# One 512-column projection per token tile in the attention heads of a hybrid encoder, in place of two of 256

## The chip, the cores and the metric

The kernel runs on one core of one Trainium2 chip. The metric is device time in microseconds (us) of one execution of the whole program; the median of several runs is compared.

## The reference

The reference is an encoder trunk of two layers on 1024 tokens of width 1024, in float32. Each layer normalises its input, projects it to 8192 columns at once, and runs three groups of heads on parts of them: four mLSTM heads, six HGRN2 heads and four differential-attention heads. Each group's output is multiplied by a SiLU gate of its own, and an output projection adds to the residual stream. The change touches the projection of the attention heads only:

```python
h = rms_norm(x, norm_g[l])
proj = jnp.einsum("bsd,de->bse", h, w_in[l])
(xm, om, zm, hq, hff, hfb, hi, hz, aq, ak, av, az) = jnp.split(proj, split_pts, axis=-1)
...
ao = differential_attention(aq..., ak..., av..., lam, positions)
ao = head_rms_norm(ao, a_norm_g[l], A_HEADS) * (1.0 - lam_init)
y_a = ao * jax.nn.silu(az)
```

An attention head takes 128 columns each of aq (two query sets of 64), ak (two key sets of 64), av (values) and az (gate). Queries and keys get a rotary embedding on 16 of their 64 dimensions. The head's weights are softmax(Q1 K1) - lam softmax(Q2 K2), and they multiply V.

## The kernel before, in words

**Precision by three products.** Float32 products are formed from a rounded part and a remainder in the type fp32r. The normalised input h lies transposed in SBUF as `hh` (high) and `hl` (low), each in two halves of 512 tokens. A weight block is fetched by `load_w` in pieces of 128x512 (DMA on SP's queue into a raw buffer, three of them), copied to `whi` by ScalarE (L136) and subtracted to `wlo` by GpSimd (L137). The pool `wp` has two slots of 2048 columns each for `whi` and `wlo`; a slot is given out again when everything that reads it is done. A block of up to 256 columns fills one slot with all eight k (k counts the 128-row pieces of the 1024 input channels). A wider block is split: k 0 to 3 in one slot, k 4 to 7 in the next.

**Token projection.** `proj_token` (L308) gives one token tile (128 tokens) of a block: 24 matmuls, 8 k times hh*whi, hh*wlo, hl*whi, the token tile as loaded weights and the block's columns as moving data. They add up in one of two PSUM banks (tag `pj`), and `evac` empties the bank.

**Attention.** After the other groups' heads, head 0's projection runs by itself. Then for each head the loop over eight query tiles `qt` computes scores S (L997, L998), the row maxima (L1000), exponentials (L1004), the combination of the two softmaxes (L1013), eight transposes (L1018), the product with V (L1025), and the gated output into the head's gate buffer (L1028). The projection of the next head is a Python generator, `a_proj`, and `next(nxt, None)` at the end of each query step takes one piece of it. Before the change it has eight pieces of two tiles each: aqk tiles 0, 1; aqk 2, 3; avz 0, 1; avz 2, 3; and the same for the second half of the tokens. With the second aqk piece of a half comes `qk_half`: rotary embedding on VectorE (L931 to L937), 16 transposes (L942), and copies to the query and key tiles `qks` (L944 to L948), from a buffer `qk` of which there is one.

**Buffers.** Values `v` (traced as av) and gates `gt` (traced as ag) have two buffers each, so head h+2 takes head h's. Head h's gate buffer is in use until `o_post`, traced in the second query step of the head after it, has normalised (L913) and transposed it (L918, L919).

**Order.** The tile framework decides, when the kernel is built, in which order each engine executes its instructions: by program order among those that its own timeline has ready. It also places the waits for slots. On the chip each engine then follows its list.

**After attention.** The output projection (L1064, traced as op) loads `w_out` through the same pool `wp`, and its y tiles through the same raw buffers. Its first three groups of channels need no attention output, and their matmuls fill in beside the softmax of head 3.

Of the kernel before, what the change touches and what calls it, by code (L numbers as in the profile page):

```python
# [13 lines left out]
AF = mybir.ActivationFunctionType  # L14
ALU = mybir.AluOpType
AX = mybir.AxisListType

P = 128
# [22 lines left out]
def _cols(start, n):  # L41
    return list(range(start, start + n))


def w_blocks():
    blocks = {}
    order = []

    def add(name, cols):
        blocks[name] = cols  # L50
        order.append(name)

    for i in range(3):
        add(("xm", i), _cols(XM + i * 256, 256))
    for j in range(6):
        add(("zm", j), _cols(ZM + j * P, P))
    for p in range(2):
        add(("om", p), _cols(OM + p * 384, 384))
    for h in range(HH):
        add(("hqf", h), _cols(HQ + h * P, P) + _cols(HFF + h * P, P))  # L60
        add(("hfb", h), _cols(HFB + h * P, P))
        add(("hiz", h), _cols(HI + h * P, P) + _cols(HZ + h * P, P))
    for h in range(AH):
        add(("aqk", h), _cols(AQ + h * P, P) + _cols(AK + h * P, P))
        add(("avz", h), _cols(AV + h * P, P) + _cols(AZ + h * P, P))
    return blocks, order


# [22 lines left out]
def trunk(ctx, tc, x_in, positions, w_in, w_out, pvec, rvec, out, dbg=None):  # L91
    nc = tc.nc
# [47 lines left out]
    def load_win(l, name):  # L140
        n = len(W_BLOCKS[name])
        o = W_OFF[name] * 8
        ks_per = 8 if n <= 256 else 4
        parts = []
        for k0 in range(0, 8, ks_per):
            hi, lo = load_w(w_in[l, :, o + k0 * n:o + (k0 + ks_per) * n], ks_per * n)
            for k in range(ks_per):
                parts.append((hi[:, k * n:(k + 1) * n], lo[:, k * n:(k + 1) * n]))
        return parts
# [197 lines left out]
    for l in range(DEPTH):  # L347
# [10 lines left out]
        h = []  # L358
# [42 lines left out]
        with tc.tile_pool(name=f"ma{l}", bufs=2) as ma:  # L401
# [38 lines left out]
            for i in range(3):  # L440
                parts = load_win(l, ("xm", i)) if l or i else xm0
                for jj in range(2):
# [3 lines left out]
                    def ev(ps, half, xm=xm):  # L446
                        nc.scalar.activation(xm[:, half * 512:(half + 1) * 512], ps, AF.Copy)
# [458 lines left out]
        with tc.tile_pool(name=f"at{l}", bufs=2) as ap, tc.tile_pool(name=f"aw{l}", bufs=1) as aw:  # L906
# [43 lines left out]
            def a_proj(hd, v, gt):  # L950
                if hd == 1:
                    sets[1] = aw.tile([P, 3, 2, S], F32R, name=f"qks{l}1", bufs=1)
                pqk = load_win(l, ("aqk", hd))
                pvz = load_win(l, ("avz", hd))

                def evv(ps, tt):
                    nc.scalar.activation(v[:, tt], ps[:, :P], AF.Copy)
                    nc.scalar.activation(gt[:, tt], ps[:, P:], AF.Tanh, scale=0.5)
                    nc.vector.scalar_tensor_tensor(gt[:, tt], gt[:, tt], 1.0, ps[:, P:], op0=ALU.add, op1=ALU.mult)  # L959
                for half in range(2):  # L960
                    qk = ap.tile([P, 4, 4, 2, QK], F32, tag="qk", name=f"qk{l}{hd}{half}", bufs=1)

                    def evqk(ps, tt, qk=qk):
                        nc.scalar.activation(qk[:, tt % 4],
                                             ps.rearrange("p (n d) -> p n d", n=4).unsqueeze(2).broadcast_to([P, 4, 2, QK]), AF.Copy)
                    for t4 in (0, 2):
                        proj_token(pqk, 2 * P, h, evqk, f"aqk{l}{hd}", [half * 4 + t4, half * 4 + t4 + 1])
                        if t4 == 2:
                            qk_half(hd, half, qk)
                        yield  # L970
                    for t4 in (0, 2):
                        proj_token(pvz, 2 * P, h, evv, f"avz{l}{hd}", [half * 4 + t4, half * 4 + t4 + 1])
                        yield

            pend = None
# [187 lines left out]
```

## Time and profile before

| | before |
|---|---|
| median of 3 runs | 2884.77 us (2881.54 to 2888.69) |
| the profiled execution | 2886.49 us |
| its span, first to last instruction | 2884.8 us |
| TensorE matmuls (PE) busy | 2795.3 us, 97% |
| weight loads (PEld) busy | 2487.5 us, 86% |
| VectorE (DVE) busy | 1850.4 us, 64% |
| ScalarE (ACT) busy | 1071.7 us, 37% |
| GpSimd (POOL) busy | 636.0 us, 22% |
| granted TensorE clock, mean | 0.990 |

The profile shows one execution. A row of a group of instructions has the line, engine, operation, tiles written and read, shapes and count, then busy time and mean duration of one, then the idle time of the engine before them and what ended it. A timeline row has start and duration in us, engine, line, operation, tiles, and how many instructions were merged into it. Matmuls overlap in their pipeline, so the distance from one start to the next, the pitch, says what a matmul costs in a stream; its duration is longer.

### The profile page before, as it was taken

To read this page: it belongs to the slowest core of one execution; us is meant where nothing else is said; L and a number is where in the kernel's file an instruction comes from. 1 tells how busy PE (TensorE), PEld (TensorE's weight loads), DVE (VectorE), ACT (ScalarE), POOL (GpSimd) and SP (SyncE) were. 2 spreads that over 40 slices of the span, in tenths; PEclk is the share of its full clock that TensorE was granted. 3 is DMA by queue.
4 is the path that set the end of the run, shared out by engine and by line. 5 is a ranking of instruction groups with operands and counts; after the bars stand their busy time and mean duration, and the time that the engine had idled before them with its cause. 6 is when DMAs were issued, how large, how long until landed. Compare 5 with 4: busy or idle time off the path is not lost. (4 is left out here: it accounts for less than half of the span.)

```text
span 2884.8 us, 49995 instructions
## 1 busy us (share of the span) xinstructions
PE 2795.3 (97%) x20004; PEld 2487.5 (86%) x20004; DVE 1850.4 (64%) x4054; ACT 1071.7 (37%) x2422; POOL 636.0 (22%) x554
## 2 busy tenths in 40 slices
PE   6999999999999999999999999999899999999998
PEld 5888888889888999988879788888798999998886
DVE  6667767566464566696566577676565536767865
ACT  4333333323333445442233323332233324545423
POOL 2122323212123111012211323132122321111112
PEclk9999999999999999999989999999999999999999
DMA  3422212211122001223324311221111221113132
GB/s 120 130 73 68 92 59 71 81 52 45 45 96 96 30 30 37 85 77 95 116 75 125 97 54 62 72 93 46 46 45 59 86 91 30 38 30 114 57 98 102
DMA packets 129864, 210.20 MB, mean 73 GB/s; under 512 B 10832, under 2 KB 60496, under 8 KB 129632
## 3 DMA queue, kind: packets, MB, share of 16 engines
q1 hardware_dynamic: 129632, 207.01, 22.1%
q8 instruction: 157, 2.57, 0.4%
q14 instruction: 75, 0.61, 0.1%
HBM read 156.58 MB, written 50.40 MB: 72 GB/s over the span
## 5 line engine op out<-in xcount | busy, mean ns | idle before, releaser
L137 POOL TENSOR_TENSOR wlo<-wraw,whi 128x512 fp32r<-128x512 f32 x320 | 443.0, 1406 | 1613.1 <-ACT whi L136 1562.0
L1064 PE MATMUL op<-whi,yb 128*128 128x512 f32 x1024 | 332.9, 398 | 0.3 <-DVE xo L1068 0.3
L136 ACT ACTIVATE whi<-wraw 128x512 fp32r<-128x512 f32 x320 | 184.4, 625 | 282.8 <-PE op L1064 83.2
L1068 DVE TENSOR_TENSOR xo<-op,xo 128x512 f32<-128x512 f32 x256 | 174.1, 687 | 94.6 <-PE op L1064 94.4
L1064 PEld LDWEIGHTS op<-whi,yb 128*128 128x128 f32 x1024 | 192.9, 188 | 44.5 <-DVE xo L1068 1.2
L308 PE MATMUL pt_hiz<-whi,hh 128*128 128x256 f32 x768 | 225.6, 294 | 2.5 <-DVE hg L680 2.5
L308 PE MATMUL pt_hiz<-whi,hl 128*128 128x256 f32 x768 | 224.6, 292 | 0.0
L308 PE MATMUL pt_hiz<-wlo,hh 128*128 128x256 f32 x768 | 223.1, 290 | 0.0
L1064 PE MATMUL op<-wlo,yb 128*128 128x512 f32 x512 | 201.9, 394 | 0.0
L1004 ACT ACTIVATE e<-S,mx 128x1024 f32<-128x1024 f32 x128 | 142.2, 1113 | 143.1 <-DVE mx L1001 77.7
L1000 DVE TENSOR_REDUCE mx<-S 128x1 f32<-128x1024 f32 x128 | 154.9, 1218 | 36.6 <-PE S L998 35.6
L645 POOL TENSOR_SCALAR ks<-xcth,wsv 128x192 f32<-128x192 f32 x112 | 108.2, 967 | 291.2 <-PE st L649 273.0
L308 PEld LDWEIGHTS pt_hiz<-whi,hh 128*128 128x128 f32 x768 | 146.7, 191 | 7.1 <-DVE hg L680 3.5
L308 PE MATMUL pt_avz<-whi,hh 128*128 128x256 f32 x512 | 147.9, 289 | 4.4 <-DVE ag L959 4.4
L308 PEld LDWEIGHTS pt_hiz<-whi,hl 128*128 128x128 f32 x768 | 146.6, 191 | 2.3 <-issue 1.0
L308 PEld LDWEIGHTS pt_hiz<-wlo,hh 128*128 128x128 f32 x768 | 146.7, 191 | 1.7 <-POOL wlo L137 0.2
L308 PE MATMUL pt_aqk<-whi,hh 128*128 128x256 f32 x512 | 146.1, 285 | 0.0
L308 PE MATMUL pt_avz<-whi,hl 128*128 128x256 f32 x512 | 146.0, 285 | 0.0
L308 PE MATMUL pt_aqk<-wlo,hh 128*128 128x256 f32 x512 | 145.9, 285 | 0.0
L308 PE MATMUL pt_avz<-wlo,hh 128*128 128x256 f32 x512 | 145.6, 284 | 0.0
L308 PE MATMUL pt_aqk<-whi,hl 128*128 128x256 f32 x512 | 145.3, 284 | 0.0
L1025 PE MATMUL po<-av,wT 128*128 128x128 f32 x1024 | 134.5, 275 | 3.4 <-DVE mx L1001 3.4
(359 smaller groups left out, 7582.9 us busy)
## 6 DMA issues: line engine op xcount, KB each, us to landing
wraw<-w_in SPq DMA_DIRECT2D x256, 256.0 KB, 2.8
wraw<-w_out SPq DMA_DIRECT2D x64, 256.0 KB, 2.7
yr<-yT SPq DMA_DIRECT2D x64, 256.0 KB, 2.9
xac<-xcd SPq DMA_DIRECT2D x16, 512.0 KB, 7.1
W<-mu SPq DMA_DIRECT2D x32, 256.0 KB, 3.6
xcd<-xc SPq DMA_DIRECT2D x12, 512.0 KB, 3.0
xct<-tka SPq DMA_DIRECT2D x12, 512.0 KB, 3.2
vd<-tkv SPq DMA_DIRECT2D x12, 512.0 KB, 3.3
```

The source lines that it names most:

```text
L136: nc.scalar.activation(hi[:, o:o + m], rw[:, :m], AF.Copy)
L137: nc.gpsimd.tensor_sub(lo[:, o:o + m], rw[:, :m], hi[:, o:o + m].bitcast(F32))
L308: nc.tensor.matmul(ps[:, :n], a[:, k, ts], b, start=(i == 0), stop=(i == 23))
L645: nc.gpsimd.tensor_scalar(ks[:, k0:k0 + MD], xct[:, c], wsv[:, d, c, hd:hd + 1], None, op0=ALU.mult)
L1000: nc.vector.tensor_reduce(mx, ps, axis=AX.X, op=ALU.max)
L1004: nc.scalar.activation(e, ps, AF.Exp, scale=QK ** -0.5, bias=mx, accum_out=ls_)
L1025: nc.tensor.matmul(po[:, :P], wT[:, t * P:(t + 1) * P], v[:, t], start=(t == 0), stop=(t == NT - 1))
L1064: nc.tensor.matmul(ps, a[:, j, ts], b[:, cs_], start=(i == 0), stop=(i == 5))
L1068: nc.vector.tensor_tensor(xv, ps, xv, op=ALU.add)
```

## The change

The two weight blocks of a head become one block of 512 columns, so each of its two slots holds four of the eight k. A token tile is projected once, to a full PSUM bank, and one evacuation takes queries and keys, values, and the gate from it. The generator has three pieces for each half of the tokens instead of four: tiles 0 and 1, tile 2, tile 3 (the last with `qk_half`). So six pieces follow the query steps 0 to 5, and steps 6 and 7 have none. The bytes loaded and the arithmetic stay as they were; the host lays out the weights accordingly.

```diff
     for h in range(AH):
-        add(("aqk", h), _cols(AQ + h * P, P) + _cols(AK + h * P, P))
-        add(("avz", h), _cols(AV + h * P, P) + _cols(AZ + h * P, P))
+        add(("aqvz", h), _cols(AQ + h * P, P) + _cols(AK + h * P, P) + _cols(AV + h * P, P) + _cols(AZ + h * P, P))
...
-                pqk = load_win(l, ("aqk", hd))
-                pvz = load_win(l, ("avz", hd))
-
-                def evv(ps, tt):
-                    nc.scalar.activation(v[:, tt], ps[:, :P], AF.Copy)
-                    nc.scalar.activation(gt[:, tt], ps[:, P:], AF.Tanh, scale=0.5)
-                    nc.vector.scalar_tensor_tensor(gt[:, tt], gt[:, tt], 1.0, ps[:, P:], op0=ALU.add, op1=ALU.mult)
+                parts = load_win(l, ("aqvz", hd))
                 for half in range(2):
...
-                    for t4 in (0, 2):
-                        proj_token(pqk, 2 * P, h, evqk, f"aqk{l}{hd}", [half * 4 + t4, half * 4 + t4 + 1])
-                        if t4 == 2:
+                    def ev(ps, tt, evqk=evqk):
+                        evqk(ps[:, :2 * P], tt)
+                        nc.scalar.activation(v[:, tt], ps[:, 2 * P:3 * P], AF.Copy)
+                        nc.scalar.activation(gt[:, tt], ps[:, 3 * P:], AF.Tanh, scale=0.5)
+                        nc.vector.scalar_tensor_tensor(gt[:, tt], gt[:, tt], 1.0, ps[:, 3 * P:], op0=ALU.add, op1=ALU.mult)
+
+                    for tiles in ((0, 1), (2,), (3,)):
+                        proj_token(parts, 4 * P, h, ev, f"aqvz{l}{hd}", [half * 4 + t for t in tiles])
+                        if tiles[0] == 3:
                             qk_half(hd, half, qk)
-                        yield
-                    for t4 in (0, 2):
-                        proj_token(pvz, 2 * P, h, evv, f"avz{l}{hd}", [half * 4 + t4, half * 4 + t4 + 1])
                         yield
```

## The prediction

> **What bounds the kernel now.** I read the page's busy times first, then the windows over one layer's attention, the groups by line, the waits of TensorE alone, and last the timelines at the seams between heads.
>
> ```profile
> PE 2795.3 (97%) x20004; PEld 2487.5 (86%) x20004; DVE 1850.4 (64%) x4054; ACT 1071.7 (37%) x2422; POOL 636.0 (22%) x554
> ```
> ```profile
> 912.38:964.50 52.12, 51.42 (x424) 50.81 (x423) 17.93 (x36) 17.39 (x42) 14.03 (x9) 1.00 0.16 52
> 964.50:1043.60 79.10, 79.10 (x622) 76.42 (x621) 53.05 (x116) 40.99 (x91) 10.86 (x8) 1.00 0.09 28
> 1043.60:1133.20 89.60, 86.65 (x678) 82.86 (x677) 60.15 (x142) 43.40 (x98) 10.23 (x8) 1.00 0.10 31
> 1133.20:1222.50 89.30, 86.34 (x679) 82.75 (x678) 59.58 (x140) 43.39 (x97) 10.25 (x8) 1.00 0.22 77
> ```
>
> The windows' columns are wall time, then busy time of PE, PEld, DVE, ACT and POOL, granted clock, DMA share and GB/s. The stretches are the four in which layer 0 projects its heads: head 0 by itself, then heads 1, 2 and 3, each beside the softmax of the head before it. PE is busy in nearly all of it, at full clock. DVE, the next engine, works 60.15 of 89.60 us. So PE sets the pace, a shorter PE stream shortens the kernel, and any hole in the stream lengthens it. The holes of one layer, by waits of PE from 912.4 to 1223 us, are these (engine and line, released by, us, times, longest):
>
> ```profile
> PE pt_avz L308 <- DVE ag L959: 2.2, 2, 1.1
> PE po L1025 <- DVE mx L1001: 1.7, 2, 0.9
> PE wT L1018 <- DVE ag L1028: 1.3, 2, 0.7
> PE qkT L942 <- DVE qk L937: 0.7, 1, 0.7
> PE qkT L942 <- ACT ayo L919: 0.7, 2, 0.3
> ```
>
> Together 6.6 us; the answer for layer 1, 2342 to 2653 us, is the same line for line. There is little idle PE time to win, and the change can add some.
>
> **The change, part 1: the matmuls.** Per token tile, head and layer, 48 matmuls of 256 columns (24 for aqk, 24 for avz) become 24 of 512. The columns streamed are the same; what goes is the fixed part of 24 instructions and the switch to a second tile. Over 8 tiles, 4 heads and 2 layers that is 64 tiles. Busy times of matmuls overlap, so I take pitches from windows of PE alone (wall, busy, clock, DMA):
>
> ```profile
> 912.38:923.97 11.59, 11.59 (x97) 1.00 0.42 137
> 918.28:923.97 5.69, 5.69 (x50) 1.00 0.77 263
> 1342.42:1348.70 6.28, 6.28 (x29) 1.00 0.52 154
> ```
>
> The first holds exactly four 256-column tiles of aqk, 96 matmuls: 11.59/4 = 2.90 us a tile. The second is its last two: 2.85 us. The third is 27 matmuls of 512 columns in the output projection, which has the same operand roles (token tile loaded, weights streamed): 6.28/27 = 0.2326 us, so 24 take 5.58 us. (The count in brackets includes neighbours that overlap the edges.) A pair of old tiles costs 5.69 to 5.80 us, a new one 5.58: a gain of 0.11 to 0.22 us. Times 64, 7 to 14 us. I take the middle, 0.16 us, that is **10 us off PE**. As PE has hardly any holes there, all of it is on the path.
>
> The Trainium skill, page "TensorE: Matmul & The Clock Gate", section "Back-to-back issue gap", gives a warm gap of N/2.4 + 2.5 ns. By it only 2.5 ns go with each of the 1536 instructions removed, an estimate of 3.8 us instead of 10. The trace does not agree: even its lower pitch leaves 2 x 118.5 - 232.6 = 4.4 ns a pair, and the rows decide.
>
> **Part 2: evacuation.** The instructions that empty PSUM are the same in kind, number and shape.
>
> ```profile
> L964 ACT ACTIVATE qk<-pt_aqk 128x512 f32<-128x512 f32 x64 | 38.2, 596 | 73.0 <-PE pt_aqk L308 66.4 <-issue 6.3
> L957 ACT ACTIVATE av<-pt_avz 128x128 f32<-128x128 f32 x64 | 17.8, 278 | 33.9 <-PE pt_avz L308 33.1
> L958 ACT ACTIVATE ag<-pt_avz 128x128 f32<-128x128 f32 x64 | 17.5, 280 | 0.0
> L959 DVE SCALAR_TENSOR_TENSOR ag<-ag,pt_avz 128x128 f32<-128x128 f32 x64 | 17.4, 282 | 11.2 <-ACT ag L958 10.3
> ```
>
> One bank now waits for all four: 596 + 278 + 280 + 282 ns = 1.4 us, where it waited 0.6 or 0.8 us. The cover is the other bank's tile, 5.58 us on PE: cost nothing. If the last of the four can't run, the cover is gone; that is part 4.
>
> **Part 3: weights.** The bytes, the DMAs (16 of 256 KB a head on SP's queue), the hi copies on ACT and the lo subtractions on POOL are unchanged. But a slot of the weight pool held one group over all eight k; now it holds k 0 to 3 or k 4 to 7 of everything, and every token tile needs both slots. Before, aqk's slot was refilled while avz's last four tiles ran (four times 2.85 = 11.4 us of cover), and avz's slot under the next head's first aqk tiles. Now the first slot comes free half a tile (2.8 us) before the head ends, the second at its end. What a refill takes, from the end of head 0's aqk (start, us, engine; first that last matmul):
>
> ```profile
> 949.50 0.28 PE L308 MATMUL pt_aqk<-whi,hl 128*128 128x256 f32 x1
> 950.32 1.66 ACT L136 ACTIVATE whi<-wraw 128x512 fp32r<-128x512 f32 x3
> 951.02 3.90 POOL L137 TENSOR_TENSOR wlo<-wraw,whi 128x512 fp32r<-128x512 f32 x3 [29.45 <-ACT whi L136]
> 955.61 1.27 POOL L137 TENSOR_TENSOR wlo<-wraw,whi 128x512 fp32r<-128x512 f32 x1 [0.69 <-ACT whi L136]
> ```
>
> All four k are ready at 956.88, 7.3 us after the release, the first of them at 952.3, 2.7 us after it. For two slots POOL adds four more subtractions, at the same pace some 6.6 us: the last k is ready 13.9 us after the first release, 11.1 us after the head's end, and the first about at its end. The next head's first two tiles (two PSUM banks) use 2 x 3 x 0.2326 = 1.4 us a k, about POOL's pace, if PE takes both tiles k by k: hole 11.1 + 1.4 - 11.2 = 1.3 us. If it does one tile first, the first ends at 11.1 + 0.7 instead of 5.6: 6.2 us. Between heads 1 and 2 and 2 and 3, softmax work covers it (part 4); between head 0 and 1 there is none yet. There a second cover falls away too:
>
> ```profile
> 951.07 1.40 DVE L934 TENSOR_TENSOR rt<-qk,sinb 128x128 f32<-128x128 f32 x1
> 952.39 2.68 DVE L936 TENSOR_TENSOR qk<-rt,rt 128x128 f32<-128x128 f32 x2
> 964.48 1.22 DVE L1000 TENSOR_REDUCE mx<-S 128x1 f32<-128x1024 f32 x1 [1.76 <-PE S L998]
> ```
>
> From the last aqk tile (949.6) over the rotary step, which takes 1.3 us an operation while POOL subtracts, and the transposes to the first reduction of scores are 14.9 us, hidden so far by avz's 11.4. In the new kernel this chain starts at the head's end and the next head's first two tiles must hide it, with the third behind them as soon as a bank is free. Bounds for this seam: 0 and 6.2 us. I take 1.5, near the lower, since PE mixes tiles and score products elsewhere in this trace (rows under the third rival); two layers, **+3 us**.
>
> At a layer's start the second slot is held until the last pc_zm matmul, just before 912.38:
>
> ```profile
> 912.40 1.67 ACT L136 ACTIVATE whi<-wraw 128x512 fp32r<-128x512 f32 x3 [5.68 <-PE pc_zm L295]
> 912.68 2.84 POOL L891 TENSOR_SCALAR xcp<-xcp,mgs 128x1024 f32<-128x1024 f32 x1 [5.31 <-PE pc_zm L295]
> 915.49 6.08 POOL L137 TENSOR_TENSOR wlo<-wraw,whi 128x512 fp32r<-128x512 f32 x4
> ```
>
> k 4 is ready at 917.0 and k 7 at 921.6. Two tiles' k 0 to 3 last until 912.4 + 5.6 = 918.0, and the rest follows the subtractions: 0. One tile first: 921.6 + 0.7 - 918.0 = 4.3 us. I take 0 by the same argument.
>
> **Part 4: the order, and the gate buffer.** Six pieces of projection follow the softmax steps 0 to 5 of the head before, in place of eight after steps 0 to 7. Steps 6 and 7 have none; PE's cover there is the next head's first tiles. These now write v and the gate at once, and gate buffers are two: head h+2's waits until head h's gated output has been normalised and transposed. Before, four aqk tiles came first, which need no gate buffer. How long it takes at heads 0 to 2:
>
> ```profile
> 1042.66 0.27 PE L308 MATMUL pt_avz<-whi,hl 128*128 128x256 f32 x1
> 1043.70 0.29 PE L308 MATMUL pt_aqk<-whi,hh 128*128 128x256 f32 x1
> 1062.59 0.35 DVE L1028 SCALAR_TENSOR_TENSOR ag<-po,r,ag 128x128 f32<-128x128 f32 x1 [0.57 <-ACT ajk L1027]
> 1082.61 0.27 ACT L958 ACTIVATE ag<-pt_avz 128x128 f32<-128x128 f32 x1
> 1084.53 0.39 PE L308 MATMUL pt_avz<-whi,hh 128*128 128x256 f32 x1 [1.11 <-DVE ag L959]
> ```
>
> Head 1's projection ends at 1042.66; head 0's last gated block is written at 1062.59; the buffer opens at 1082.61, 20 us later. In those 40 us PE had 4 aqk and 2 avz tiles, 6 x 2.85 = 17.1 us, and still came to a wait (the 1.11 us). Now it has two tiles, 11.2 us: 5.9 us less to do beside the softmax. Upper bound: 5.9 us a seam. Lower: the waits behind this buffer go, 2.2 us a layer, or -1.1 us a seam. For a value near the lower: with less projection ahead of it, PE gets to head 0's last products sooner, and the 20 us shrink. Against it: DVE and ACT must do their steps in that time. I take +1.2 us; two such seams a layer, two layers: **+5 us**.
>
> The Trainium skill, page "Perfetto Trace Analysis", section "Optimization Strategy", reads a gap that repeats on the engine that should be saturated as a sign that there is no room to allocate the next tile. The trace agrees: the wait above has the same length at both such seams of a layer (2.2 us, 2 times, longest 1.1). The rule speaks against a change that brings the tile to be allocated forward.
>
> **Part 5: the output projection's start.** Its first weights went into aqk's slot during head 3's avz tiles:
>
> ```profile
> 1206.32 1.29 POOL L137 TENSOR_TENSOR wlo<-wraw,whi 128x512 fp32r<-128x512 f32 x1 [0.86 <-ACT whi L136]
> 1224.66 0.39 PE L1064 MATMUL op<-whi,yb 128*128 128x512 f32 x1
> ```
>
> They were ready at 1207.6, 17 us ahead of their use. Now they are ready 7.3 - 2.8 = 4.5 us after head 3's end, and the y tiles' loads share raw buffers with them. The first use was 2.3 us after that end: late by 2 us or more, at most by another refill, 7.3. PE has head 2's steps 6 and 7 meanwhile. Bounds 0 and 7.3, I take 1: **+2 us** in two layers.
>
> **Sum.** -10 + 3 + 0 + 5 + 2 = 0. The profiled execution took 2886.49 us (span 2884.8), 1.7 more than the median 2884.77. I forecast 2884 us against that median, rounding down. What a measurement of this kernel can tell from no change is about 0.3%, 8.7 us.
>
> **Rivals.**
>
> *The plain gain.* Holes do not grow; PE is 97% busy and softmax work is always ready. The gain is 10 us with all holes kept (2884.8 - 10 = 2875) and 14 + 4.4 = 18 us with the largest pitch gain and the gate waits gone (2866). For it: the two-tile reading of the refill leaves hardly a hole, and the present waits are one microsecond each. Against it: three covers of 11 us are removed at once. Chance 0.34.
>
> *The gate buffer stops PE.* Slower: at each of the four seams PE fills both banks and then has only DVE-paced softmax steps until the buffer opens. Price: 4 x 5.9 = 24 us, with parts 3 and 5 as above 2884.8 - 10 + 24 + 5 = 2904. It decides when a seam costs over (8.7 + 10 - 5)/4 = 3.4 us. For it: the buffer already opens late today, 20 us after its last writer, and DVE is 67% busy in these windows. Against it: attention steps of the next head can fill PE, since their scores are ready earlier. Chance 0.17.
>
> *One tile at a time.* If PE's order is fixed so that a tile's second half waits for the refill with nothing between, the two lone seams of a layer cost 6.2 + 4.3 us, 21 us in all instead of 3: 2884 + 18 = 2902. For it: the order on PE is set when the kernel is built, not when k is ready. Against it: single score products already stand between projection matmuls, so the order is finely mixed:
>
> ```profile
> 1044.54 0.28 PE L308 MATMUL pt_aqk<-wlo,hh 128*128 128x256 f32 x1
> 1044.66 0.40 PE L997 MATMUL S<-qks 128*128 128x512 f32 x1
> 1044.90 0.28 PE L308 MATMUL pt_aqk<-whi,hl 128*128 128x256 f32 x1
> ```
>
> Chance 0.07.
>
> *No gain per matmul* is the case in which 512 columns cost twice 256; the lower row (0.11 us a tile, 7 us) excludes it.
>
> **Numbers.** Likeliest, the gain and the holes about cancel (2876 to 2893): 0.42. Faster by over 0.3%: the plain gain, 0.34. Slower by over 0.3%: 0.17 + 0.07 = 0.24. The range goes from 2868, near the end of the plain gain, to 2901, just short of the slow rivals' full prices.
>
> **What would show it.** Matmuls of pt_aqvz number 1536 in three groups of 512 at about 0.2326 us pitch: part 1. The first hi copies of a head right after, or within 3 us before, the last projection matmul of the head before, and lo subtractions 8 in a row: part 3. Waits of PE by the gate's multiply (L959's successor) well above 1.1 us each: part 4; if these exceed 3.4 us a seam, the forecast is wrong upwards. A first op matmul more than 3 us after the last projection: part 5. If total PE waits in a layer stay near 6.6 us, the plain gain holds and I am wrong downwards.

## The result, and the profile after

| | before | after |
|---|---|---|
| median | 2886.27 us | 2952.2 us (2949.79 to 2953.66) |
| span of the profiled execution | 2884.8 us | 2951.6 us |
| granted TensorE clock, mean | 0.990 | 0.990 |

The ratio is 1.0227, with a 95% interval of 1.0215 to 1.0240: the change makes the kernel 66 us slower. The forecast was 2884 us with a range up to 2901.

The page's busy times of the kernel after, and its windows over the projections of layer 0's four heads (columns as before):

```profile
PE 2812.9 (95%) x18468; PEld 2407.0 (82%) x18468; DVE 1852.0 (63%) x4054; ACT 1066.2 (36%) x2422; POOL 641.3 (22%) x554
```
```profile
909.20:958.90 49.70, 48.46 (x213) 38.22 (x212) 10.44 (x23) 12.87 (x33) 10.53 (x7) 1.00 0.10 33
958.90:1038.20 79.30, 74.38 (x390) 61.12 (x389) 48.41 (x104) 36.65 (x81) 11.83 (x10) 1.00 0.09 29
1038.20:1134.80 96.60, 89.46 (x486) 73.97 (x485) 54.27 (x134) 42.08 (x96) 10.45 (x9) 0.98 0.09 28
1134.80:1232.40 97.60, 90.42 (x489) 74.38 (x488) 58.46 (x140) 43.00 (x98) 10.23 (x9) 0.98 0.20 70
```

TensorE has 1536 instructions fewer, as the change says. The wall time of a window less PE's busy time gives the holes: 1.2, 4.9, 7.1 and 7.2 us for heads 0 to 3, where the kernel before had 0.7, 0, 3.0 and 3.0. Heads 2 and 3 also show a granted clock under 1.00. The same account in wall time, from the first projection matmul of layer 0 to the last matmul of each head's projection, then to the last transposes of attention output, then to the last matmul of the output projection (us, from the timelines):

| | head 0 | head 1 | head 2 | head 3 | to last transposes | to end of output projection | sum |
|---|---|---|---|---|---|---|---|
| before | 51.3 | 79.0 | 89.6 | 90.0 | 109.6 | 113.0 | 532.5 |
| after | 49.7 | 79.3 | 96.6 | 97.7 | 135.5 | 104.5 | 563.2 |

Layer 0 loses 30.7 us here and layer 1, by the same account, 29.3 (532.3 to 561.6): 60 of the 66 us; the rest is in the stages around. Half of it lies in heads 2 and 3 (14.7), half behind the last projection (17.4), and nothing at heads 0 and 1 (1.3 us less than before). The waits of TensorE in layer 0 of the kernel after, 909.2 to 1472.3 us, longest groups:

```profile
PE po L1021 <- DVE mx L997: 5.6, 4, 2.0
PE op L1060 <- DVE xo L1064: 4.2, 7, 1.2
PE S L993 <- ACT e L1000: 3.5, 4, 1.2
PE wT L1014 <- DVE qks L947: 3.4, 6, 1.1
PE pt_aqvz L307 <- DVE ag L963: 3.1, 3, 1.2
```

The gate's own row is the last of them and small. The rows above it are TensorE waiting on softmax steps and on the residual sum of the output projection. Here a blocked projection seldom shows as a wait *of the projection*: other work stands before it in TensorE's list, and the holes are put down to that work. The projection's own instructions show where it stopped.

**Where it stopped.** Three places in layer 0, by timeline. First, head 1's tiles 4 and 5: the rotary step of the first half ends at 992.6, its transposes come 21 us later, and the next copies to the query-and-key buffer wait for them (the first two rows are the buffer's instructions grouped, with min/median/max ns and first and last start; then the timeline):

```profile
L936 DVE TENSOR_TENSOR qk<-rt,rt x2: 280/280/281, 992.4 to 992.6; 128x128 f32<-128x128 f32 x2
L941 PE MATMUL qkT<-ident,qk x16: 271/272/328, 1013.4 to 1018.0; 128*128 128x128 f32 x16
```
```profile
1009.08 0.39 PE L307 MATMUL pt_aqvz<-whi,hl 128*128 128x512 f32 x1
1019.78 0.61 ACT L957 ACTIVATE qk<-pt_aqvz 128x512 f32<-128x512 f32 x1
1020.57 0.64 ACT L957 ACTIVATE qk<-pt_aqvz 128x512 f32<-128x512 f32 x1
1023.72 0.39 PE L307 MATMUL pt_aqvz<-whi,hh 128*128 128x512 f32 x1
```

Both banks are full from 1009 until 1020, and no projection matmul runs from 1009.1 to 1023.7. In the kernel before, four tiles of avz stood between the last aqk tile of a half and the first of the next, so the one buffer had time to empty: the same transposes were done 8 us before the next copy, and that copy waited for TensorE's tile alone.

```profile
L942 PE MATMUL qkT<-ident,qk x16: 270/272/274, 989.8 to 998.6; 128*128 128x128 f32 x16
1006.86 0.60 ACT L964 ACTIVATE qk<-pt_aqk 128x512 f32<-128x512 f32 x1 [0.75 <-PE pt_aqk L308]
```

Second, head 2's first two tiles end at 1056.1 and fill both banks:

```profile
1056.10 0.39 PE L307 MATMUL pt_aqvz<-whi,hl 128*128 128x512 f32 x1
1059.57 1.08 ACT L957 ACTIVATE qk<-pt_aqvz 128x512 f32<-128x512 f32 x2
1071.39 0.45 ACT L961 ACTIVATE av<-pt_aqvz 128x128 f32<-128x128 f32 x2
1072.55 0.35 DVE L1024 SCALAR_TENSOR_TENSOR ag<-po,r,ag 128x128 f32<-128x128 f32 x1
1081.68 1.96 PE L1021 MATMUL po<-av,wT 128*128 128x128 f32 x8 [1.93 <-DVE mx L997]
1087.36 0.43 ACT L962 ACTIVATE ag<-pt_aqvz 128x128 f32<-128x128 f32 x2
1089.84 0.48 PE L307 MATMUL pt_aqvz<-whi,hh 128*128 128x512 f32 x1
```

A bank is emptied in three steps, each when its buffer opens: queries and keys first, values 12 us after them, the gate 28 us after them. The row at 1072.55 is the last use of the gate buffer by softmax, head 0's last gated block; the buffer opens 15 us behind it. The next tile starts at 1089.84, 34 us after the last one. In that stretch TensorE has softmax alone, and VectorE sets its pace. The windows of this stop and of head 3's:

```profile
1056.10:1089.80 33.70, 27.74 (x169) 22.57 (x168) 28.41 (x74) 18.84 (x42) 0.00 (x0) 0.95 0.02 8
1153.80:1187.50 33.70, 27.70 (x171) 22.39 (x169) 28.02 (x74) 18.80 (x42) 0.00 (x0) 0.95 0.02 8
```

Each has 6.0 us without PE, DVE is 83 to 84% busy, and the mean clock of the stretch is 0.95.

Third, the end of head 3's projection:

```profile
1232.43 0.40 PE L307 MATMUL pt_aqvz<-whi,hl 128*128 128x512 f32 x1
1235.78 0.48 PE L1060 MATMUL op<-whi,yb 128*128 128x512 f32 x1
1256.60 1.21 DVE L996 TENSOR_REDUCE mx<-S 128x1 f32<-128x1024 f32 x1
```

The last of these is head 3's first row maximum. It comes 24 us after the projection ends, since the last tile of it still holds keys that every score needs. In between lie the rotary step, the transposes and copies behind head 2's last softmax steps. Before, the aqk tiles of head 3 ended four avz tiles earlier, and that maximum came 2.9 us after the projection's end:

```profile
1222.26 0.29 PE L308 MATMUL pt_avz<-whi,hl 128*128 128x256 f32 x1
1225.14 1.22 DVE L1000 TENSOR_REDUCE mx<-S 128x1 f32<-128x1024 f32 x1
```

So the last softmax starts 31 us later in the run. TensorE is not idle meanwhile:

```profile
1232.40:1256.60 24.20, 22.80 (x121) 17.70 (x120) 22.54 (x43) 16.07 (x32) 8.08 (x6) 1.00 0.44 138
```

It has head 2's last softmax steps and early output matmuls. These are then missing beside head 3's softmax: from the projection's end to the last transposes the pitches exceed those of a stream by 12.3 us, where they did by 2.5 before. (For each matmul this takes what its pitch has beyond the usual one of its kind, and adds that up; the figure moves by up to 1 us with what is taken as usual.)

### The profile page after: what moved, and what is told of

Read it like the earlier page. It is cut to its first block, busy times and chain, and to the rows that moved or that the text cites. A ratio compares the mean times of both kernels' runs of the same rounds, so it can differ in the third digit from the quotient of the medians.

```text
span 2951.6 us, 46910 instructions
## 1 busy us (share of the span) xinstructions
PE 2812.9 (95%) x18468; PEld 2407.0 (82%) x18468; DVE 1852.0 (63%) x4054; ACT 1066.2 (36%) x2422; POOL 641.3 (22%) x554
## 5 line engine op out<-in xcount | busy, mean ns | idle before, releaser
L307 PE MATMUL pt_aqvz<-whi,hh 128*128 128x512 f32 x512 | 203.1, 401 | 7.3 <-DVE ag L963 7.3
L307 PE MATMUL pt_aqvz<-wlo,hh 128*128 128x512 f32 x512 | 203.3, 398 | 0.0
L307 PE MATMUL pt_aqvz<-whi,hl 128*128 128x512 f32 x512 | 202.4, 395 | 0.0
L1021 PEld LDWEIGHTS po<-av,wT 128*128 128x128 f32 x1024 | 128.2, 192 | 22.7 <-DVE mx L997 12.7
L779 DVE TENSOR_TENSOR ks<-ks,T 128x1024 f32<-128x1024 f32 x84 | 123.4, 1469 | 17.2 <-PE lv L760 16.8
L638 ACT ACTIVATE n<-num,ginter 128x193 f32<-128x193 f32 x112 | 47.3, 422 | 218.1 <-PE num L637 190.9
```

What stands on the lines that cost most here:

```text
L307: nc.tensor.matmul(ps[:, :n], a[:, k, ts], b, start=(i == 0), stop=(i == 23))
L638: nc.scalar.activation(n, pi, AF.Copy, scale=ginter[:, d, c, hd:hd + 1])
L779: nc.vector.tensor_tensor(kv, kv, tk, op=ALU.mult)
L1021: nc.tensor.matmul(po[:, :P], wT[:, t * P:(t + 1) * P], v[:, t], start=(t == 0), stop=(t == NT - 1))
```

## Experiments

Medians, with the ratio to the kernel before of the same runs (its medians were 2886.6 to 2888.1 us) and its 95% interval. The theories are: the gate and value buffers (**G**), the one query-and-key buffer (**K**), the piece count (**P**), the order with queries and keys last, so that nothing of the projection hides the way from them to the first scores, the "bare end" (**Q**), and the weight slots (**W**).

**Buffers for values and gates, after the change (G).**

```diff
-v = ap.tile(..., name=f"av{l}{hd}"), gt = ap.tile(..., name=f"ag{l}{hd}")
+v = ap.tile(..., name=f"av{l}{hd}", bufs=3), gt = ap.tile(..., name=f"ag{l}{hd}", bufs=3)
```

> The changed kernel with three buffers instead of two for the values and for the gates of an attention head, nothing else. Three theories of the 66 us. G, the buffers: the next head's first tile can't be emptied from PSUM until the head before the last has released its gate (and value) buffer, so TensorE loses its projection work for some 30 us at two seams a layer. It expects most of the loss back: 2875 to 2905 us. P, the pieces: softmax steps 6 and 7 have no projection beside them. It expects less than 10 us back, 2940 to 2955. W, the weight slots: both slots are needed by every tile, and they are refilled only at a head's end. It expects the same as P, 2940 to 2955.

2936.0 us, 1.0170 (1.0155 to 1.0186): 16 us of the 66. Layer 0's heads 2 and 3 take 93.5 and 93.5 us instead of 96.6 and 97.7. The buffers are a cause, and not the main one.

**Eight pieces of one tile (P).**

```diff
-for tiles in ((0, 1), (2,), (3,)):
+for tiles in ((0,), (1,), (2,), (3,)):
```

> The changed kernel with eight pieces of one tile, after all eight softmax steps, instead of six pieces. P expects most of the 66 us back, 2885 to 2910. G expects 2940 to 2955, since the first two tiles fill both PSUM banks as before and wait for the same buffer. W expects 2940 to 2960, as the refill still comes at a head's end, now with less softmax work behind it.

2959.0 us, 1.0250 (1.0235 to 1.0266): 7 us slower still. The six pieces aren't what costs.

**Six pieces in the kernel before (P).** The four aqk tiles of a half in one piece, avz as it was.

```diff
-for t4 in (0, 2):
-    proj_token(pqk, ..., [half * 4 + t4, half * 4 + t4 + 1]) ...
+proj_token(pqk, ..., [half * 4 + t for t in range(4)])
+qk_half(hd, half, qk)
+yield
```

> The kernel before (two blocks of 256 columns, own slots, the gate needed only by avz) with six pieces: aqk's four tiles of a half in one piece, avz's in two, so that steps 6 and 7 have none. P expects it 30 to 60 us slower than before, 2915 to 2945. G and W expect it within 12 us of before, 2875 to 2898, because neither the moment the gate is needed nor the slots have changed much.

2914.5 us, 1.0096 (1.0080 to 1.0111). Lumping pieces costs the old order 28 us; by what means was not followed. It doesn't carry over: in the fused kernel eight pieces are no better than six.

**The kernel before with avz ahead of aqk (G and Q together, nothing fused).** The edit also loads avz's weights first.

```diff
 for half in range(2):
+    for t4 in (0, 2):
+        proj_token(pvz, 2 * P, h, evv, ...); yield
     for t4 in (0, 2):
         proj_token(pqk, 2 * P, h, evqk, ...)
         if t4 == 2:
             qk_half(hd, half, qk)
         yield
-    for t4 in (0, 2):
-        proj_token(pvz, 2 * P, h, evv, ...); yield
```

> The kernel before with avz's two pieces ahead of aqk's in each half, so that the first tile of a head needs the value and gate buffers at once, as in the changed kernel; 256-column matmuls, eight pieces and own slots stay. G expects 30 to 60 us slower than before, 2915 to 2945. P and W expect it within 12 us of before, though the chain from queries and keys to the first scores of head 0 is now bare at its end, which may cost up to 10 us in two layers.

2952.6 us, 1.0226 (1.0209 to 1.0243): the whole loss, to within a microsecond, without one 512-column product. Heads 2 and 3 take 104.7 and 99.9 us. So the order alone can cost 66 us. That it is the same number is chance: four avz tiles still lie between the two uses of the query-and-key buffer here, so K has no part in it, and heads 2 and 3 lose more than in the fused kernel. Nor do the parts add up: the two edits further down that make one half of this change each cost 23 and 14 us.

**A second query-and-key buffer, after the change (K), and with it a third gate buffer (K and G).**

```diff
-qk = ap.tile([P, 4, 4, 2, QK], F32, tag="qk", ..., bufs=1)
+qk = ap.tile([P, 4, 4, 2, QK], F32, tag="qk", ..., bufs=2)
```

> The changed kernel with two instead of one of the buffers that hold a half's queries and keys before their transposes. Theory K: tile 4 of a head can't be emptied until the 16 transposes of tiles 0 to 3 have read the one buffer, and these stand behind softmax products in two shared PSUM banks, some 20 us after the rotary step in the trace of the changed kernel; both projection banks are full meanwhile. K expects 15 to 35 us back, 2917 to 2937. Theory Q, the bare end: the chain from a head's last queries and keys to the next head's first scores has no projection behind it, so softmax starts late and TensorE runs short later. It expects less than 8 us back, 2944 to 2955. Theory G, the gate and value buffers, which gave 16 us by themselves, expects the same as Q.

> The changed kernel with two query-and-key buffers and three gate buffers (a third value buffer does not fit beside them). K and G together expect most of the loss back, 2880 to 2905. Q expects 2920 to 2940: the gate's 16 us and little more.

2928.6 us, 1.0141 (1.0124 to 1.0158), and with the third gate buffer 2914.0 us, 1.0090 (1.0075 to 1.0105). The second buffer is worth 24 us, more than the gate's. Head 1 was as long after the change as before it (79.3 and 79.0 us), so the table above doesn't show this loss; its window in the kernel with two query-and-key buffers has hardly a hole left:

```profile
957.90:1024.40 66.50, 66.24 (x333) 54.90 (x333) 38.71 (x85) 30.99 (x69) 10.36 (x9) 1.00 0.11 32
```

66.5 us where it took 79.3. Part of this is lost again at head 2, which reaches the closed gate buffer earlier and takes 102.9 us instead of 96.6. With the gate buffer added, head 2's stop shows what is late next, in ScalarE's timeline:

```profile
1042.07 0.60 ACT L957 ACTIVATE qk<-pt_aqvz 128x512 f32<-128x512 f32 x1 [1.02 <-PE pt_aqvz L307]
1069.09 0.28 ACT L961 ACTIVATE av<-pt_aqvz 128x128 f32<-128x128 f32 x1
1069.24 0.29 ACT L962 ACTIVATE ag<-pt_aqvz 128x128 f32<-128x128 f32 x1
```

The gate goes out right behind the values, 27 us after queries and keys, so what is late now is the values' buffer. (No run has a third values buffer together with these two, so this reading is not tested.)

**Only the second half's order turned, in the kernel before (Q).** avz, then aqk in tiles 4 to 7.

> The kernel before, with the order of aqk and avz exchanged in the second half of a head's tokens only: the head ends with aqk, its rotary step and its transposes, with nothing of the projection behind them. Gate first needed after four aqk tiles, as before; eight avz tiles lie between the two uses of the query-and-key buffer. Q expects 20 to 50 us slower than before, 2907 to 2937. K and G expect it within 12 us of before, 2875 to 2899.

2911.5 us, 1.0083 (1.0068 to 1.0098): the bare end costs 23 us by itself, in the old order. Head 3's first row maximum comes 19 us after its projection's end.

**Only the first values and gates brought forward, in the kernel before (G).** avz 0, 1; aqk 0 to 3; avz 2, 3; the second half as it was.

> The kernel before, in the order avz tiles 0, 1, aqk 0 to 3, avz 2, 3, aqk 4 to 7, avz 4 to 7: the value and gate buffers are needed by the first tile, but the head ends with avz tiles as before. Two avz tiles lie between the uses of the query-and-key buffer, where there were four. G expects 20 to 45 us slower than before, 2907 to 2932. Q expects it within 12 us of before. K expects 5 to 15 us slower, as half of that buffer's cover is gone.

2902.4 us, 1.0048 (1.0033 to 1.0063): 14 us, about what the third gate buffer gave back in the fused kernel (14.6 beside K). The cover of the query-and-key buffer is halved here too, two avz tiles in place of four, so G is not quite alone in this edit.

**Weights laid out as after, matmuls and order as before (W).**

```diff
-pqk = load_win(l, ("aqk", hd)); pvz = load_win(l, ("avz", hd))
+parts = load_win(l, ("aqvz", hd))
+pqk = [(a[:, :2 * P], b[:, :2 * P]) for a, b in parts]
+pvz = [(a[:, 2 * P:], b[:, 2 * P:]) for a, b in parts]
```

> The kernel before, in its order and with 256-column matmuls, but with the weights of a head laid out as in the changed kernel: k 0 to 3 of all 512 columns in one slot, k 4 to 7 in the other, so that every tile needs both slots and they are refilled only at a head's end. Theory W, the refill, expects 10 to 30 us slower than before, 2897 to 2917. K, G and Q, which together already account for the 66 us, expect it within 9 us of before, 2879 to 2897.

2918.3 us, 1.0111 (1.0096 to 1.0126): 32 us. Here the refill shows as a wait, in the first two heads of layer 0 (907 to 1046 us):

```profile
PE pt_aqk L307 <- POOL wlo L136: 2.7, 6, 1.2
```

TensorE's waits of the kernel after have no row of this kind. An estimate from the pitches makes this plausible: two 256-column tiles taken together use up a k in 2 x 3 x 0.1185 = 0.71 us, two of 512 columns in 1.4, and GpSimd's subtractions took about 1.3 us for each. But the waits in this row are a small part of the 32 us. The attention stages of both layers lose 21.6 us of them, the other stages the rest, and what makes up the difference was not followed.

**Half and half.** After the change with two query-and-key and three gate buffers; tiles 0 to 3 fused, one tile a piece; tiles 4 to 7 in the old order, aqk first, from the same weights.

> The changed kernel with two query-and-key buffers and three gate buffers, and with the second half of a head's tokens projected as before: 256 columns for aqk's four tiles, then 256 columns for avz's, in four pieces; the first half stays at 512 columns, in four pieces of one tile. The head's end is covered by avz tiles again. Q expects some 20 us less than the 2914 us of the kernel with those buffers alone, less half of the gain per matmul: 2888 to 2900. If Q is wrong and pieces or slots hold the rest, it stays at 2908 to 2920.

2886.0 us, 0.9999 (0.9990 to 1.0009): with the bare end mended too, the loss is gone. Head 3's first row maximum comes 11 us after its projection's end, in place of 24 after the change, and of 39 in the fused kernel with the same buffers. (The second half is narrow here as well as in the old order; no run parts the two.)

**The same buffers in the kernel before.**

> The kernel before with three value and three gate buffers. Its waits of TensorE behind the gate's multiply are 2.2 us a layer. G expects 2 to 8 us less than before, 2879 to 2885; the others expect no change, 2884 to 2890.

> The kernel before with two query-and-key buffers and three gate buffers. K expects no gain from the first, since avz tiles lie between its uses, and G 2 to 8 us from the second: 2877 to 2887. The order of work may change by itself; then anything within 10 us.

2904.0 us, 1.0064 (1.0049 to 1.0079), and 2902.8 us, 1.0060 (1.0045 to 1.0075). More buffers made the old kernel 16 to 17 us *slower*. What costs is seen at the start of the attention stage; it is read below, where a later run shows it best.

**Eight pieces with the mended buffers, and smaller weight slots.** The first is the kernel with two query-and-key and three gate buffers and one-tile pieces. The next three have four weight slots of 1024 columns in place of two of 2048, in the same memory: the fused kernel with mended buffers, the half-and-half kernel, and the kernel before.

```diff
-lo = wp.tile([P, 2048], F32R, tag="wlo", ...); hi = wp.tile([P, 2048], F32R, tag="whi", ...)
+lo = wp.tile([P, 1024], F32R, tag="wlo", ..., bufs=4); hi = wp.tile([P, 1024], F32R, tag="whi", ..., bufs=4)
-ks_per = 8 if n <= 256 else 4
+ks_per = 8 if n <= 128 else 4 if n <= 256 else 2
```

> The changed kernel with two query-and-key buffers, three gate buffers and eight pieces of one tile, all at 512 columns; it differs from the half-fused kernel only in the second half of a head's tokens. Q, the bare end of a head, expects that the pieces do not help: 2906 to 2925. P, the pieces, expects most of the 28 us: 2884 to 2897.

> The changed kernel with two query-and-key buffers, three gate buffers and four weight slots of 1024 columns in place of two of 2048, in the same memory: a slot comes free after a quarter of a tile's matmuls, and the refill of the next head starts 4.2 instead of 2.8 us before a head's end. The output projection and all other blocks use the small slots too. W, the refill, expects 10 to 25 us less than 2914: 2889 to 2904. Q expects within 8 us of it: 2906 to 2922.

> The half-fused kernel (first half of a head's tokens at 512 columns, second half at 256 with avz last) with the four small weight slots. W expects 5 to 15 us less than 2886, below the kernel before: 2871 to 2881. If the refill is hidden in it already, 2880 to 2892.

> The kernel before with the four small weight slots, the control: there every slot already has 11 us to be refilled in, so W expects no change from that in the attention heads, 2880 to 2890; elsewhere the order may change by up to 10 us either way.

2923.8 us, 1.0133 (1.0119 to 1.0148): one-tile pieces cost 10 us here as well. Small slots: 2899.3 us, 1.0038 (1.0025 to 1.0051), 15 us better than with large ones; half and half 2866.7 us, **0.9928 (0.9916 to 0.9941)**, 19 us better and faster than both kernels; before 2883.5 us, 0.9986 (0.9978 to 0.9995). Little of the gain of small slots is in the attention stage. Half and half takes 529.2 us there in layer 0, against 532.4 with large slots (layer 1: 530.4 against 532.1), but 887.0 against 898.1 from there to layer 1's attention. Most of it lies in the other stages, whose projections share the pool. So about 5 us of the fastest kernel's lead on the kernel before lie in its attention stages (1059.6 us in two layers, against 1064.8), the rest in stages that the fusing doesn't touch. Yet the slots alone, in the kernel before, gave only 4 us; why they give more beside the new order was not followed.

**The width alone, and the buffers and slots alone.** From the fastest kernel: its fused tiles split in two 256-column products again, all else kept; and the kernel before with that kernel's buffers and slots.

```diff
-proj_token(parts, 4 * P, h, ev, f"aqvz{l}{hd}", [t])
+proj_token(pqk, 2 * P, h, evqk, f"aqk{l}{hd}", [t])
+proj_token(pvz, 2 * P, h, evv, f"avz{l}{hd}", [t])
```

> The fastest kernel so far (first half of a head fused in one-tile pieces, second half as before, two query-and-key buffers, three gate buffers, four small weight slots; 2866.7 us), with one thing taken back: the four tiles of a head's first half are projected in two products of 256 columns each, query-and-key and then value-and-gate, with the same weights in the same places, the same pieces and the same buffers. If the width of the product is what is left of the gain, 4 tiles x 4 heads x 2 layers = 32 tiles each lose about 8 x (2 x 0.1185 - 0.2326) = 0.04 us, some 1 us, and 32 more copies out of PSUM appear that stand beside the matmuls: 2866 to 2872 us. If one wide PSUM bank a tile is what lets the next tile start (one copy to wait for, not two), it is slower by more than 10 us: over 2876 us. If the wide bank is what holds the softmax products out of PSUM, it is faster: under 2862 us.

> The kernel before in its own order, with everything that the fastest kernel has beside the fusing: two query-and-key buffers, three gate buffers and four small weight slots. If buffers and slots alone make the gain and fusing the first half gives nothing, it comes to 2860 to 2872 us. If the fusing of the first half with its one-tile pieces is needed, it stays near what the buffers alone gave in this order (2902.8 us) less what the small slots gave (3.3 us): 2890 to 2905 us.

2898.4 us, 1.0048 (1.0034 to 1.0063), and 2887.7 us, 1.0004 (0.9996 to 1.0013). Without the width the gain is gone and more: 32 us, the case for which the expectation named the wide bank. The attention stages lose 23.3 us of the 32; the other 8.4 lie in stages that this edit leaves as they are, so a difference of this size can come from a changed order alone, which is worth keeping in mind beside the smaller ones above. And buffers and slots without the fusing leave the old kernel where it was, 21 us above the fastest. The matmuls don't explain it. (The working in that expectation counted 8 matmuls a tile. There are 24, so 24 x (2 x 0.1185 - 0.2326) = 0.11 us a tile and 3.4 us in 32 tiles, still a tenth of what was measured.) The trace shows a good part of it at the start of the stage. ScalarE's waits of the 256-column version, 910 to 918.5 us, then TensorE's timeline and its windows:

```profile
ACT qk L959 <- DMA yT<-xcp: 8.8, 1, 8.8
```
```profile
913.70 0.28 PE L307 MATMUL pt_avz<-whi,hl 128*128 128x256 f32 x1
918.34 0.58 PE L307 MATMUL pt_aqk<-whi,hh 128*128 128x256 f32 x1 [4.36 <-ACT qk L959]
918.72 0.41 PE L307 MATMUL pt_aqk<-wlo,hh 128*128 128x256 f32 x1
918.93 0.41 PE L307 MATMUL pt_aqk<-whi,hl 128*128 128x256 f32 x1
```
```profile
913.70:918.30 4.60, 0.28 (x3) 0.07 (x1) 0.44 (x1) 0.61 (x2) 0.00 (x0) 0.85 0.54 188
918.30:923.60 5.30, 5.26 (x24) 5.26 (x25) 0.29 (x1) 0.32 (x2) 0.00 (x0) 0.50 0.00 2
```

The first query-and-key copy of the stage waits for a DMA that still reads `xcp`, a tile of the stage before, so the memory of that tile must have gone to one of the new ones. Both banks are full after 5.7 us, TensorE stops for 4.4 us, and its next tile runs at half clock: 0.213 us a matmul instead of 0.1185, 24 x 0.095 = 2.3 us more. In the fastest kernel the same DMA is issued as late (912.78, 6.7 us after the stage's first matmul; 914.17 and 6.1 us here) and lands at 916.40, but there it stops nothing. TensorE mixes the stage's first two tiles (a row with x2 is the same product of both), so neither is done earlier:

```profile
915.77 0.63 PE L307 MATMUL pt_aqvz<-wlo,hh 128*128 128x512 f32 x2
916.23 0.63 PE L307 MATMUL pt_aqvz<-whi,hl 128*128 128x512 f32 x2
916.79 0.60 ACT L959 ACTIVATE qk<-pt_aqvz 128x512 f32<-128x512 f32 x1 [9.80 <-PE pt_aqvz L307]
```

The first tile's last matmul starts at 916.23, and its copy follows at once, released by TensorE. Two wide banks hold 11.2 us of work, enough to reach past the DMA, and TensorE waits for 0.5 us in this stretch. So a good part of the wide product's worth in this kernel is how far TensorE can run ahead before a bank must be emptied. With half clock the stop is some 7 us in layer 0 and 5 in layer 1 (head 0 takes 56.9 and 55.2 us instead of 49.9 and 50.0), 12 of the 32 us. Head 1 of the 256-column version takes 6.4 and 7.5 us longer in the two layers; refill waits are there, but only 1.6 and 2.1 us, and part comes back in head 2. The rest is spread.

The kernel before with added buffers has the same stop, in all three versions. With two query-and-key buffers, three gate buffers and small slots, TensorE's wait is

```profile
PE pt_aqk L308 <- ACT qk L964: 4.9, 1, 4.9
```

in layer 0 and 5.5 us in layer 1, with ScalarE again held by that DMA. With large slots head 0's holes grew from 1.6 us in each layer to 8.5 and 7.3 (pitches beyond those of a stream), 12.6 us, beside the 16 that the same buffers cost in all. In the kernel before the same DMA is issued at 919.1 and lands 3.1 us later, and the first copies, from 915.5 on, don't wait for it. So what cost this, it seems, is not the number of the buffers but the place that their memory came from; no run gives the same buffers other memory.

## Why the prediction was wrong

**Right.** Part 1: in a stream of the kernel after the starts stand at

```profile
957.22 0.39 PE L307 MATMUL pt_aqvz<-wlo,hh 128*128 128x512 f32 x1
...
959.77 0.40 PE L307 MATMUL pt_aqvz<-whi,hh 128*128 128x512 f32 x1
```

eleven pitches, 0.232 us each. The mean pitch of all projection matmuls of layer 0, holes left out, is 0.2324 us for 768 of them, where it was 0.1190 for 1536: 178.5 us instead of 182.8, or some 8 us in two layers, where 10 were taken. (The Trainium skill, page "TensorE: Matmul & The Clock Gate", section "Back-to-back issue gap", gives the formula that part 1 quotes for an isolated matmul. The pitches here are those of a stream, so they don't speak against it, and its 3.8 us was no estimate for this case.) Part 3's description held as well. The first hi copies came within 3 us before a head's end, and eight lo subtractions ran in a row:

```profile
L135 ACT ACTIVATE whi<-wraw x8: 615/632/632, 956.5 to 967.5; 128x512 fp32r<-128x512 f32 x8
L136 POOL TENSOR_TENSOR wlo<-wraw,whi x8: 1284/1294/1452, 957.2 to 968.3; 128x512 fp32r<-128x512 f32 x8
```

and no wait of TensorE in this layer's list is put down to them. The price put on that seam, 3 us, came to nothing for TensorE: with K mended, the pitches of heads 0 and 1 exceed those of a stream by 2.7 us in all, by 3.4 before. The layer start's 0 held. Part 5 gave 1 us a layer; the first output matmul came 3.4 us after the end instead of 2.3.

**Mis-sized: part 4.** It took 1.2 us a seam. The third gate buffer gives back 14.6 us on top of K, that is 3.7 us for each of four seams, and with a third values buffer but without K 16.2 us, 4.0 a seam. The windows agree: the holes of heads 2 and 3 grew by 4.1 and 4.2 us. The hole in each stop, 6.0 us, is nearly the 5.9 us named as the upper bound. (The 6.0 are all of a stop's holes, though, and not only the new ones, so that agreement is partly chance.) The choice between the bounds failed: it was argued that TensorE would reach head 0's last products sooner. It reached them later. Head 0's last gated block is written 34 us after head 1's projection ends (1072.55 and 1038.2), where it was 20 us (1062.59 and 1042.66). Only the way from there to the open buffer shrank, from 20 to 15 us. TensorE had run out of projection, and softmax ran at VectorE's pace, having started late itself: head 0's first row maximum came 15 us after the end of its projection, where it came 0.8 us after it. Of the rivals, the gate buffer's mechanism was right; its price of 24 us was too high for this term and far too low for the change.

The Trainium skill's rule that the prediction weighed here ("Perfetto Trace Analysis", "Optimization Strategy": a repeated gap can mean that there is no room for the next tile) pointed the right way: the stop repeats at 33.70 us in heads 2 and 3, and a third buffer takes part of it away.

**Missing: the query-and-key buffer.** Here the prediction failed in part 2, which put evacuation at "cost nothing". It says of evacuation that the other bank's tile covers it, and names the one `qk` buffer where it describes the code, but it asks only of the gate buffer when it opens. The four avz tiles between the two halves were the cover of this buffer. The change removes them; no projection matmul then starts for 14.6 us in head 1 (1009.1 to 1023.7), and a second buffer is worth 24 us.

**Missing: the bare end at every head.** "A second cover falls away" was seen and priced at the seam of head 0 to 1 alone, within 3 us. It was set aside for the other heads because softmax work covers them. That work covers TensorE, but the next head's softmax starts late all the same, and at the last head nothing is left behind which to hide it. Turning the order of the second half alone costs 23 us in the kernel before; restoring it, with narrow tiles, in the mended kernel gives 28 (2914.0 to 2886.0).

In order of repair: 2952.2, 2928.6 (K), 2914.0 (G), 2886.0 (the old second half, with its pieces). The prices hold for this order of repair; they don't add up freely, and that they end at the kernel before to a microsecond is chance. The weight layout costs 32 us in the old order and none can be seen for it in half and half. What the rest of these interactions is was not settled: the order on each engine is fixed when the kernel is built, and an edit can change it far from its own lines.

## What to carry to other kernels

When two projections are fused, list every buffer that either one's evacuation writes, and for each the work that used to stand between its last reader and its next writer. Put what the next stage needs first at the front of the order and what can wait at the end; fuse only where that order stays. When buffers are added, look at which tile's memory they take over and who still reads it. And read a stop from the blocked instructions' own timeline, since the waits are booked on whatever the engine did instead.

## What the hardware showed that was not expected

- A hole of 4.4 us costs more than itself: the granted clock was 0.50 for the 5.3 us after it, and 24 matmuls of 256 columns took 0.213 us each instead of 0.1185. The Trainium skill, page "TensorE: Matmul & The Clock Gate", section "What's actually happening", describes a half-rate clock after an idle window of about 3.4 us; the run after the 4.4 us hole agrees. But TensorE need not be idle for that long at a stretch. In head 2's stop of the kernel after, the longest hole was 1.9 us; TensorE was busy for 1.47 us of 3.40, and ran the next 3.40 at half clock. This is what brings the mean of the stop to 0.95:

```profile
1078.40:1081.80 3.40, 1.47 (x14) 1.28 (x13) 3.37 (x10) 0.81 (x1) 0.00 (x0) 1.00 0.00 0
1081.80:1085.20 3.40, 3.40 (x13) 2.91 (x14) 3.19 (x17) 1.94 (x6) 0.00 (x0) 0.51 0.00 0
```

- A new stage's tile can have to wait for the old stage's readers, where it seems to have got their memory: the DMA of a y tile of the stage before held up the first copy of the attention stage by 4 us (its tile's matmuls were done at 913.7, it ran at 917.7) in kernels with added buffers and 256-column tiles. In the kernel before, the first copies wait for TensorE alone.
